# Two of four weight sums of a down projection made by copies and adding transfers in DRAM, on one core of a Trainium2 chip

## The chip, the cores and the metric

The kernel runs on one core of one Trainium2 chip. Its engines work in parallel, each through its own list of instructions in a fixed order: TensorE (PE, matrix products, with weight loads shown as PEld), VectorE (DVE), ScalarE (ACT), GpSimd (POOL) and SyncE (SP), which here does nothing but issue DMA transfers. DMA moves data between DRAM and the on-chip memory SBUF; matrix products end in PSUM, whose eight buffers are called banks. Engines wait for one another and for transfers through semaphores.

The metric is the device time of one execution in microseconds (us). Before the change it is 1109.34 us, the median of three runs (1109.31 to 1109.88).

## What is computed

One encoder block: RMSNorm, two kinds of attention (8 heads each), an output projection with residual, and a gated MLP with a small convolution, for 256 tokens and 16 meta tokens, model width 2048, MLP width 5632. All in float32. The part that the change touches is the last product, `@ w_down`:

```python
def conv_glu(x, w_gate, w_up, conv_w, conv_b, w_down):
    g = x @ w_gate
    u = x @ w_up
    ...
    gc = conv_b
    for i in range(CONV_W):
        gc = gc + conv_w[i] * gp[:, i:i + L]
    return (jax.nn.silu(gc) * u) @ w_down

def reference(x, meta_tokens, ...):
    ...
    mix = jnp.concatenate([rmsnorm(out_a, na_out_g[l]), rmsnorm(out_b, mla_out_g[l])], axis=-1)
    h = h + mix @ w_out[l]
    h = h + conv_glu(rmsnorm(h, ffn_norm_g[l]), w_gate[l], w_up[l], conv_w[l], conv_b[l], w_down[l])
    return h[:, N_META:]
```

## The kernel before

**Precision.** Each float32 operand is split into a rounded part `hi` (ACT, `split_hi`) and a rest `lo` (DVE, `split_lo`), and a product is made of three: hi·hi, hi·lo, lo·hi. So every block of weights costs one ACT and one DVE instruction before PE can use it.

**The stream of weights.** `pieces` is the list of all weight pieces in the order of use, mostly 128x1024 float32 (512 KB). `load_weights` issues their loads on SP in this order, as buffers come free: five buffers `raw` (one more, `more_raw`, in the MLP), four `whi`, four `wlo`. The pieces that belong to the scheme of seven products have their own larger buffers, two called `quarters` for the weights and two for their sums (`sums4`; these tiles carry the name quarters in the profile as well).

**The order of work.** There is no scheduler on the chip. The class `Flow` plays the whole kernel through once while it is built: each step is a generator that yields an engine and an estimated cost in ns, waits for an `Event`, or takes a buffer from `Slots`. The step that can start first is written down next. The order in which each engine's instructions are written is the order in which that engine runs them. Costs of the plan thus decide order alone; on the chip, an engine whose next instruction is not ready holds everything behind it. `load` issues a transfer and plans its end from bytes / 350 per ns, one after another, plus 2000 ns for landing.

**Stages in time.** Input and latent projections and the attention run to about 290 us, where heads of both kinds are interleaved with the projections of the next; the output projection follows (to about 400 us), then gate and up projections with their scheme of seven products (to about 870 us), then the down projection.

**POOL in the attention.** It does small things: the rest part of the meta columns of each softmax row (`meta_copies`, tile p, line 266), the split of small sums (sq8r), rotary products (kr, scr), copies of small queries (qs), and running sums of squares (sum_a, sum_b, kr). In the output projection it adds the residual (res).

**Seven products.** Half of the down projection's columns (SF = 1024) are computed by a scheme of the Strassen–Winograd kind: for each pair of 128-row blocks of the weights (`RowPair`, 22 of them) a 2x2 block product is made from seven products instead of eight. The four blocks of the weights lie in the order B11, B12, B22, B21 in `w_down_s` (512 columns each). The products 3, 2 and 1 use raw blocks; 5, 7, 6 and 4 use four sums of blocks, 512 columns each, made in `weight_sums` by DVE: the first two in one instruction of 128x1024, the other two in one of 128x512 each. `load_pair` takes a `quarters` buffer and loads the pair's 1 MB in two transfers of 512 KB, then the sums of activations (`s_down`, tile `sin`). The up projection uses the same class with a quarter of the width (q = 256 columns).

`Quarters.there` says when a piece can be split: raw pieces after `loaded`, the first two sums after `summed[0]`, the other two after `summed[1]`. A raw buffer is free again when its pieces are split and the sums made (`used("raw")`).

Of the kernel before, what the change touches and what calls it, by code (L numbers as in the profile page):

```python
# [35 lines left out]
FC = D_FF // P  # L36
# [19 lines left out]


AHEAD, BEHIND = 3, 8

# [146 lines left out]
def encoder_block(ctx: ExitStack, tc: tile.TileContext, io):  # L206
    nc = tc.nc
    ctx.enter_context(tc.manual_schedule())
    fl = Flow()
# [12 lines left out]
    def size(ap):  # L222
        n = 1
        for s in ap.shape[1:]:
            n *= s
        return n
# [13 lines left out]
    def TT(out, a, b, op):  # L240
        yield "dve", 68 + 1.04 * size(out)
        nc.vector.tensor_tensor(out, a, b, op)  # L242
# [54 lines left out]
    def one(slots):  # L297
        (t,) = yield slots, 1
        return t
# [6 lines left out]
    PW = 1024  # L306
# [89 lines left out]
    pieces = []  # L396
# [44 lines left out]
    for w, f in enumerate(QUADS):  # L441

        g, end = f // 2, (*QUADS, FC)[w + 1] // 2
# [4 lines left out]
        for i in range(KC // 2):  # L448
            r = RowPair(io["w_up_s"][w][i], i, PW // 4)
# [7 lines left out]
        for i, u in enumerate(scheme):  # L457
            a, b = (j * len(middle) // len(scheme) for j in (i, i + 1))
# [9 lines left out]
    for g in range(FC // 2):  # L468
        r = RowPair(io["w_down_s"][g], g, PW // 2)
# [13 lines left out]
    def load(out, src, ev, queue):  # L483

        nc_bytes = 4 * P * size(out)
        t = max(dma_free[0], fl.cur.t) + nc_bytes / 350.0
        dma_free[0] = t
        queue.dma_start(out, src)
        fl.set(ev, t + 2000.0 - fl.cur.t)
# [14 lines left out]
    def load_pair(r):  # L504
        if r.of == "up":
            r.raw, r.sums = yield raws, 2
        else:
            r.raw = yield from one(quarters)
        def load_S():
            if r.near:  # L510
                r.ev_S = ev_near[r.g]
                return
            r.S = yield from one(s_parts)
            src, saved = saved_sums[r.of][r.g]
            yield saved
            yield "sp", 600
            load(r.S, src, r.ev_S, nc.sync)

        if r.of == "up":
            yield from load_S()  # L520
        for a in range(0, 4 * r.q, PW):
            yield "sp", 600
            ev = r.loaded if a + PW == 4 * r.q else Event()
            load(r.raw[:, a : a + PW], r.src[:, a : a + PW], ev, nc.sync)
        if r.of == "down":
            yield from load_S()
        fl.spawn(weight_sums(r), (lambda: 0) if r.of == "up" else 2)

    def weight_sums(r):
        yield r.loaded  # L530
        if r.of == "down":
            r.sums = yield from one(sums4)
        t, raw, q = r.sums, r.raw, r.q
        yield from TT(t[:, : 2 * q], raw[:, q : 3 * q], raw[:, : 2 * q], ALU.subtract)
        fl.set(r.summed[0])
        yield from TT(t[:, 2 * q : 3 * q], raw[:, 2 * q : 3 * q], t[:, :q], ALU.subtract)
        yield from TT(t[:, 3 * q :], t[:, 2 * q : 3 * q], raw[:, 3 * q :], ALU.subtract)
        fl.set(r.summed[1])
        r.used("raw")

# [97 lines left out]
    dpool = ctx.enter_context(tc.tile_pool(name="dpool", bufs=1, space=bass.MemoryType.DRAM))  # L638
# [3 lines left out]
    }  # L642


    late = [hpool.tile([P, 2, L], F32R, tag=f"late{i}", name=f"late{i}") for i in range(8)]
    hT = [None] * KC
    s_2 = hpool.tile([P, 288], F32, name="s_2")
# [9 lines left out]
    def first_loads():  # L657
        k, first = 0, pieces[0]
        for n, weights in ((1, 1), (1, 1), (2, 2), (3, 2), (2, 1), (2, 1), (4, 2)):
            t = x_tiles[k // 8][:, k % 8 : k % 8 + n]  # L660
            yield "sp", 450
            ev = Event()
            load(t, io["xT"][:, k : k + n, :], ev, nc.sync)
            for i in range(n):
                xt[k], x_gain[k], ev_x[k] = t[:, i, :L], t[:, i, L:], ev
                k += 1
                fl.set(ev_xt[k - 1])
            if k == 1:
# [12 lines left out]
        yield "sp", 600  # L681
        load(ident, io["ident"], ev_consts, nc.sync)
        yield "sp", 600
        load(mb, io["meta_bias"], Event(), nc.sync)

    def load_residual():
        yield ev_ob[HEADS - 1]
# [291 lines left out]
    for h in range(HEADS):  # L979
        t = apool.tile([P, 2, NT], F32R, name=f"ob{h}")  # L980
        ob.append((t[:, 0, :], t[:, 1, :]))
        t = apool.tile([P, 2, NT], F32R, name=f"oa{h}") if h < 6 else hl[KC - HEADS + h]
# [817 lines left out]
    def value_sums(dst, saved, a, b, place=None):  # L1800

        (A11, A21), (A12, A22) = ((t[:, :P], t[:, P:SEQ]) for t in (a, b))

        yield from TT(A22, A21, A22, ALU.add)
        yield from TT(A21, A11, A21, ALU.subtract)
        yield from TT(A11, A22, A11, ALU.subtract)
        yield from TT(A12, A12, A11, ALU.subtract)
        parts = place
        if place is None:
            parts = yield from one(combined)  # L1810
        hl_ = parts.bitcast(F32R).rearrange("p (i t) -> p i t", i=4)
# [101 lines left out]
    sums7, sum_banks = {}, {}  # L1913
# [52 lines left out]
    def quad_out(f, P7, b):  # L1966

        out = yield from one(raws)
        U = [[out[:, (2 * i + j) * 2 * P : (2 * i + j + 1) * 2 * P] for j in range(2)] for i in range(2)]
        m = yield mts, 2  # L1970
        c, u3 = (t[:, :SEQ] for t in m)
        yield from ACT(c, P7[1], AF.Copy)
        yield from TT(U[0][0], P7[2], c, ALU.add)
        yield from TT(c, P7[6], c, ALU.add)
        yield from TT(u3, P7[7], c, ALU.add)
        fl.put(acc, b[2])
        yield from TT(U[0][1], P7[5], c, ALU.add)
        yield from TT(U[0][1], P7[3], U[0][1], ALU.add)
        fl.put(acc, b[0])
        yield from TT(U[1][1], P7[5], u3, ALU.add)  # L1980
        fl.put(acc, b[1])
        yield from TT(U[1][0], u3, P7[4], ALU.subtract)
        fl.put(acc, b[3])
        for t in m:
            fl.put(mts, t)
        for j in range(2):
            pt = yield from one(acc)
            yield from TR(
                [(pt[:, (2 * t + i) * P : (2 * t + i + 1) * P], U[i][j][:, t * P : (t + 1) * P])
                 for t in range(2) for i in range(2)]  # L1990
            )
# [15 lines left out]
    def scheme_out(sums7):  # L2007
        t = yield from one(sums4)
        c1, u2, u3 = (t[:, i * PW // 2 : (i + 1) * PW // 2] for i in range(3))
        outs = yield quarters, 2  # L2010
        C = [[o[:, j * SF // 2 : (j + 1) * SF // 2] for j in range(2)] for o in outs]

        def done(i, j):
            for k in range(2):
                o = C[i][j][:, k * 2 * P : (k + 1) * 2 * P]
                yield from ACT(o, o, AF.Copy, scale=s_2t[:, i : i + 1])
                yield from PTT(o, o, res[2 * j + k][:, i, :], ALU.add)
            yield "sp", 600
            nc.sync.dma_start(io["out"][i][:, j * SF // 2 : (j + 1) * SF // 2], C[i][j])

        yield from ACT(c1, sums7[1], AF.Copy)
        fl.put(acc, sums7[1])
        yield from TT(C[0][0], sums7[2], c1, ALU.add)
        fl.put(acc, sums7[2])
        fl.spawn(done(0, 0))
        yield from TT(u2, sums7[6], c1, ALU.add)
        fl.put(acc, sums7[6])
        yield from TT(u3, sums7[7], u2, ALU.add)
        fl.put(acc, sums7[7])
        yield from TT(C[0][1], sums7[5], u2, ALU.add)  # L2030
        yield from TT(C[0][1], sums7[3], C[0][1], ALU.add)
        fl.put(acc, sums7[3])
        fl.spawn(done(0, 1))
        yield from TT(C[1][1], sums7[5], u3, ALU.add)
        fl.put(acc, sums7[5])
        fl.spawn(done(1, 1))
        yield from TT(C[1][0], u3, sums7[4], ALU.subtract)
        fl.put(acc, sums7[4])
        fl.spawn(done(1, 0))

# [170 lines left out]
```

## Time and profile before

| | before |
|---|---|
| median of three runs | 1109.34 us |
| span of the profiled execution, first to last instruction | 1106.7 us |
| TensorE clock granted, mean | 1.000 |
| moved by DMA | 239.41 MB, 216 GB/s on average |
| ACT busy, POOL busy | 735.1 us, 140.0 us |
| 128x1024 sums of `quarters` on DVE | 22 |
| 128x512 sums of `quarters` on DVE | 44 |

The profile gives the span and not the device time of the execution it was taken from, so the difference to the median, 2.6 us, is what lies around the span.

How to read it: a group of instructions is named by source line, engine, operation and `out<-in`; `x22` is a count, then come the busy time and the mean duration of one, then the idle time of that engine just before the group and what ended it. Many operations are recorded in helpers, so that a line alone (238 for ACT, 242 for DVE, 266 for POOL, 278 for PE) says little and the tile names tell which step it is. Matmuls overlap and their ends are modelled, so PE's busy time says that work was queued, and only the spacing of the starts tells the pace. A view of waits names, for each engine, whom it waited for, with the total time, the number of times and the longest one.

### The profile page before, as it was taken

The numbers are of one execution on the slowest core, as the hardware profiler recorded it, in microseconds if no ns is written. First come the engines' busy times: TensorE is split into PE (matmuls) and PEld (weight loads), VectorE is DVE, ScalarE is ACT, GpSimd is POOL, SyncE is SP. The second block draws the span as 40 slices with busy tenths as digits, with TensorE's granted clock in tenths as the row PEclk, the third lists the DMA queues.
The fourth block names the chain that finished last, engine by engine and source line by source line (L and its number), as shares of the span: only waits on it lengthen the run. The fifth ranks groups of instructions, "written<-read, shape, count | busy, mean of one in ns | idle before, by whom it ended". The sixth has DMA issues, their size and how long they took to land.

```text
span 1106.7 us, 22544 instructions
## 1 busy us (share of the span) xinstructions
PE 1100.6 (99%) x8414; PEld 1061.8 (96%) x8414; DVE 990.8 (90%) x1837; ACT 735.1 (66%) x1470; POOL 140.0 (13%) x202
## 2 busy tenths in 40 slices
PE   9999999999999999999999999999999999999998
PEld 9999999999999999999999999999999988888888
DVE  8979888888878989999999999988988999999984
ACT  8788979798647776656666565665565565655663
POOL 3211222121433400000000000000000011100114
PEclk9999999999999999999999999999999999999999
DMA  9553434444665796657667577777688787777772
GB/s 323 199 172 124 148 127 151 139 163 134 230 188 161 207 343 229 198 181 243 224 193 230 179 248 241 238 229 244 203 275 299 260 299 250 251 258 266 281 249 77
DMA packets 72374, 239.41 MB, mean 216 GB/s; under 512 B 8136, under 2 KB 12744, under 8 KB 72264
## 3 DMA queue, kind: packets, MB, share of 16 engines
q1 hardware_dynamic: 71976, 237.69, 63.8%
q8 instruction: 66, 1.08, 0.4%
q14 instruction: 44, 0.36, 0.1%
q10 hardware_dynamic: 288, 0.27, 0.1%
HBM read 219.44 MB, written 17.83 MB: 214 GB/s over the span
## 4 chain that ended last, share of the span: by engine, by line
PE 90%; ACT 4%; DVE 3%; issue 1%; DMA 1%; POOL 0%; DVEq 0%; POOLq 0%; ACTq 0%
PE bank L278 24%; PE bank L606 18%; PE bank L607 18%; PE bank L608 18%; PE bank L1870 6%; PE bank L1871 3%; PE bank L284 2%; ACT whi L238 1%; ACT scr L238 1%; DVE wlo L242 1%; DVE scr L250 1%; DMA raw<-in_w_cq 1%; ACT qraw L238 0%; ACT bank L238 0%; DVE cols L258 0%
## 5 line engine op out<-in xcount | busy, mean ns | idle before, releaser
L238 ACT ACTIVATE whi<-raw 128x512 fp32r<-128x512 f32 (+2 forms) x479 | 358.1, 764 | 173.2 <-PE bank L607 83.5
L242 DVE TENSOR_TENSOR wlo<-raw,whi 128x512 fp32r<-128x512 f32 (+2 forms) x479 | 414.9, 885 | 43.2 <-ACT whi L238 42.1
L606 PE MATMUL bank<-hl,whi 128*128 128x258 f32 (+2 forms) x1528 | 438.5, 287 | 0.1
L607 PE MATMUL bank<-hl,whi 128*128 128x258 f32 (+2 forms) x1528 | 433.7, 284 | 0.0
L608 PE MATMUL bank<-hl,wlo 128*128 128x258 f32 (+2 forms) x1528 | 433.0, 283 | 0.2 <-DVE wlo L242 0.2
L608 PEld LDWEIGHTS bank<-hl,wlo 128*128 128x128 f32 x1528 | 290.1, 190 | 0.9 <-DVE wlo L242 0.7
L607 PEld LDWEIGHTS bank<-hl,whi 128*128 128x128 f32 x1528 | 289.6, 190 | 0.1
L606 PEld LDWEIGHTS bank<-hl,whi 128*128 128x128 f32 x1528 | 288.6, 189 | 0.5 <-ACT scr L238 0.3
L238 ACT ACTIVATE whi<-quarters 128x1024 fp32r<-128x1024 f32 x88 | 81.5, 950 | 64.8 <-PE bank L1870 46.0
L278 PE MATMUL bank<-whi,act 128*128 128x256 f32 (+1 forms) x420 | 111.5, 317 | 0.0
L1870 PE MATMUL bank<-act,whi 128*128 128x512 f32 x308 | 110.1, 397 | 0.0
L242 DVE TENSOR_TENSOR wlo<-quarters,whi 128x1024 fp32r<-128x1024 f32 x88 | 99.4, 1156 | 10.8 <-ACT whi L238 10.2
L266 POOL TENSOR_TENSOR mt<-mt,mt 128x256 f32<-128x256 f32 x7 | 6.8, 979 | 652.4 <-ACT mt L238 652.4
L1871 PE MATMUL bank<-act,wlo 128*128 128x256 f32 x308 | 86.4, 281 | 0.0
L278 PE MATMUL bank<-whi,sin 128*128 128x512 f32 (+1 forms) x272 | 83.5, 355 | 0.0
L278 PEld LDWEIGHTS bank<-whi,act 128*128 128x128 f32 x420 | 74.1, 189 | 5.7
L1870 PEld LDWEIGHTS bank<-act,whi 128*128 128x128 f32 x308 | 57.8, 188 | 13.9
L278 PE MATMUL bank<-whi,hl 128*128 128x256 f32 x288 | 66.5, 280 | 0.0
L278 PE MATMUL bank<-wlo,act 128*128 128x256 f32 (+1 forms) x210 | 66.3, 315 | 0.0
L238 ACT ACTIVATE whi<-more_raw 128x1024 fp32r<-128x1024 f32 (+2 forms) x46 | 44.1, 962 | 24.4 <-PE bank L607 9.9
L1871 PEld LDWEIGHTS bank<-act,wlo 128*128 128x128 f32 x308 | 58.1, 189 | 1.6
L278 PEld LDWEIGHTS bank<-whi,sin 128*128 128x128 f32 x272 | 49.5, 188 | 7.7
(278 smaller groups left out, 1947.9 us busy)
## 6 DMA issues: line engine op xcount, KB each, us to landing
raw<-in_w_gate SPq DMA_DIRECT2D x83, 512.0 KB, 5.0
raw<-in_w_in SPq DMA_DIRECT2D x52, 512.0 KB, 3.9
raw<-in_w_up_s SPq DMA_DIRECT2D x44, 512.0 KB, 4.9
quarters<-in_w_down_s SPq DMA_DIRECT2D x44, 512.0 KB, 6.9
raw<-in_w_up SPq DMA_DIRECT2D x34, 512.0 KB, 5.5
raw<-in_w_out SPq DMA_DIRECT2D x32, 512.0 KB, 4.0
raw<-in_w_down SPq DMA_DIRECT2D x32, 512.0 KB, 5.2
s_down<-sums SPq DMA_DIRECT2D x22, 512.0 KB, 4.1
```

The source lines that it names most:

```text
L238: nc.scalar.activation(out, in_, f, **kw)
L242: nc.vector.tensor_tensor(out, a, b, op)
L250: nc.vector.scalar_tensor_tensor(out, a, s, b, op0, op1)
L266: nc.gpsimd.tensor_tensor(out, a, b, op)
L278: nc.tensor.matmul(o, l, r, start=start, stop=stop)
L284: nc.tensor.transpose(o, i, ident[:n, :n])
L606: nc.tensor.matmul(ps, whi, xhi, start=start, stop=False)
L607: nc.tensor.matmul(ps, whi, xlo, start=False, stop=False)
L608: nc.tensor.matmul(ps, wlo, xhi, start=False, stop=stop)
L1870: nc.tensor.matmul(ps, whi, x, start=start, stop=False)
L1871: nc.tensor.matmul(ps[:, :n], wlo, x[:, 0, :], start=False, stop=stop)
```

## The change

The first two of the four weight sums of each row pair of the down projection are no longer made on DVE. During the attention, `sums_in_dram` copies the first two blocks (B11, B12) of each pair from DRAM to a DRAM tile `early` (SP's queue, 512 KB), waits for the copy, and then adds the next two (B12, B22) to it by an adding transfer issued from POOL, DRAM to DRAM (512 KB). It starts when weight piece 18 has landed and is paced by the constants 2000, 1000 and `PACE` = 5000 ns of the plan.

In the down projection, `load_pair` loads B11 (256 KB) and B22, B21 (512 KB), leaves B12 out, and `weight_sums` loads the two finished sums (512 KB) into the sums buffer through SP once that buffer is free. The other two sums are still made on DVE, from these.

An adding transfer can only add, so the signs of the scheme are turned: the sums of weights become additions, and a few operations on activations and on the results swap add and subtract. This holds for the up projection too, whose four sums stay on DVE.

```diff
+PACE = 5000.0
...
-        for a in range(0, 4 * r.q, PW):
+        q = r.q
+        for a, b in ((0, q), (2 * q, 4 * q)) if r.of == "down" else ((0, 4 * q),):
             yield "sp", 600
-            ev = r.loaded if a + PW == 4 * r.q else Event()
-            load(r.raw[:, a : a + PW], r.src[:, a : a + PW], ev, nc.sync)
+            ev = r.loaded if b == 4 * q else Event()
+            load(r.raw[:, a:b], r.src[:, a:b], ev, nc.sync)
...
         t, raw, q = r.sums, r.raw, r.q
-        yield from TT(t[:, : 2 * q], raw[:, q : 3 * q], raw[:, : 2 * q], ALU.subtract)
-        fl.set(r.summed[0])
-        yield from TT(t[:, 2 * q : 3 * q], raw[:, 2 * q : 3 * q], t[:, :q], ALU.subtract)
-        yield from TT(t[:, 3 * q :], t[:, 2 * q : 3 * q], raw[:, 3 * q :], ALU.subtract)
+        if r.of == "down":
+            yield early_sums[r.g][1]
+            yield "sp", 600
+            load(t[:, : 2 * q], early_sums[r.g][0], r.summed[0], nc.sync)
+            yield r.summed[0]
+        else:
+            yield from TT(t[:, : 2 * q], raw[:, q : 3 * q], raw[:, : 2 * q], ALU.add)
+            fl.set(r.summed[0])
+        yield from TT(t[:, 2 * q : 3 * q], raw[:, 2 * q : 3 * q], t[:, :q], ALU.add)
+        yield from TT(t[:, 3 * q :], t[:, 2 * q : 3 * q], raw[:, 3 * q :], ALU.add)
         fl.set(r.summed[1])
         r.used("raw")
...
+    early_sums = [
+        (dpool.tile([P, PW], F32, name=f"early{g}"), Event()) for g in range(FC // 2)
+    ]
+
+    def sums_in_dram():
+        for g, (t, done) in enumerate(early_sums):
+            src = io["w_down_s"][g]
+            yield "sp", 600
+            ev = Event()
+            load(t, src[:, :PW], ev, nc.sync)
+            fl.cur.t = ev.time + 2000.0
+            yield "pool", 1000
+            nc.gpsimd.dma_start(t, src[:, PW // 2 : 3 * PW // 2], accum_op=ALU.add)
+            fl.set(done, 6000.0)
+            fl.cur.t += PACE
...
         load(mb, io["meta_bias"], Event(), nc.sync)
+        yield pieces[18].loaded
+        fl.spawn(sums_in_dram())
...
-        yield from TT(A22, A21, A22, ALU.add)
+        yield from TT(A22, A21, A22, ALU.subtract)
...
-        yield from TT(A12, A12, A11, ALU.subtract)
+        yield from TT(A12, A12, A11, ALU.add)
...
-        yield from TT(U[0][1], P7[5], c, ALU.add)
+        yield from TT(U[0][1], P7[5], c, ALU.subtract)
...
-        yield from TT(U[1][1], P7[5], u3, ALU.add)
+        yield from TT(U[1][1], P7[5], u3, ALU.subtract)
...
-        yield from TT(U[1][0], u3, P7[4], ALU.subtract)
+        yield from TT(U[1][0], u3, P7[4], ALU.add)
```

The last three edits stand in the same way in the function that puts the down projection's results together.

More of the change, by code (lines that the diff above doesn't have):

```diff
@@ L2029, in scheme_out @@
         fl.put(acc, sums7[7])
-        yield from TT(C[0][1], sums7[5], u2, ALU.add)
+        yield from TT(C[0][1], sums7[5], u2, ALU.subtract)
         yield from TT(C[0][1], sums7[3], C[0][1], ALU.add)
@@ L2033, in scheme_out @@
         fl.spawn(done(0, 1))
-        yield from TT(C[1][1], sums7[5], u3, ALU.add)
+        yield from TT(C[1][1], sums7[5], u3, ALU.subtract)
         fl.put(acc, sums7[5])
         fl.spawn(done(1, 1))
-        yield from TT(C[1][0], u3, sums7[4], ALU.subtract)
+        yield from TT(C[1][0], u3, sums7[4], ALU.add)
         fl.put(acc, sums7[4])
```

## The prediction, made before the changed kernel was run

> **What bounds the kernel now.** I read the page first, then a table by stage, then who the matrix engine waits for.
>
> ```profile
> span 1106.7 us, 22544 instructions
> PE 1100.6 (99%) x8414; PEld 1061.8 (96%) x8414; DVE 990.8 (90%) x1837; ACT 735.1 (66%) x1470; POOL 140.0 (13%) x202
> PE 90%; ACT 4%; DVE 3%; issue 1%; DMA 1%; POOL 0%; DVEq 0%; POOLq 0%; ACTq 0%
> ```
>
> PE is busy for 99% of the span and makes up 90% of the chain that ended last; VectorE (DVE) is second at 90%. The sums that the change takes away are DVE work, so the question is whether PE ever waits for DVE where they stand. The table by stage (columns: window, its length, then busy time and instruction count of PE, PEld, DVE, ACT and POOL, clock, DMA share, GB/s) has the attention from 65 to 290, the output projection's first part to 345, the gated MLP to 875, the down projection to 1075 and the tail.
>
> ```profile
> 65.00:290.00 225.00, 224.14 (x1851) 221.05 (x1850) 199.70 (x537) 196.14 (x611) 47.99 (x99) 1.00 0.46 150
> 290.00:345.00 55.00, 55.00 (x458) 55.00 (x458) 41.59 (x70) 28.92 (x55) 17.82 (x20) 1.00 0.53 172
> 345.00:875.00 530.00, 530.00 (x4430) 529.54 (x4429) 491.57 (x912) 331.39 (x535) 20.90 (x14) 1.00 0.71 234
> 875.00:1075.00 200.00, 200.00 (x1000) 168.17 (x999) 189.12 (x196) 116.69 (x138) 23.43 (x18) 1.00 0.75 265
> 1075.00:1107.00 32.00, 27.80 (x194) 25.76 (x192) 15.82 (x19) 13.77 (x21) 11.18 (x11) 1.00 0.25 83
> ```
>
> In the down projection DVE is busy for 189 of 200 us, yet PE is busy for all 200. Busy PE is modelled, so the timeline (start, duration) has to confirm it:
>
> ```profile
> 1077.33 0.40 PE L1870 MATMUL bank<-act,whi 128*128 128x512 f32 x1
> ...
> 1077.56 0.28 PE L1871 MATMUL bank<-act,wlo 128*128 128x256 f32 x1
> ...
> 1077.67 0.40 PE L1870 MATMUL bank<-act,whi 128*128 128x512 f32 x1
> ```
>
> A 512-column product starts 0.23 us and a 256-column one 0.11 us before the next: 0.45 ns a column, in step. The waits of PE and of its weight loads in the whole run (total, times, longest):
>
> ```profile
> PE bank L698 <- DVE em L695: 1.1, 1, 1.1
> PE bank L278 <- POOL sq8r L266: 0.5, 2, 0.3
> PE bank L608 <- DVE wlo L242: 0.2, 1, 0.2
> ```
> ```profile
> PEld bank L278 <- POOL sq8r L266: 1.0, 3, 0.4
> PEld bank L278 <- DVE scr L250: 0.5, 2, 0.3
> ...
> PEld bank L284 <- POOL p L266: 0.3, 1, 0.3
> ```
>
> PE waited for DVE's split weights (wlo) for 0.2 us in all. What it does wait for in the attention is mostly POOL. So the removed work lies under a saturated PE, and the added work is issued from the engine that PE is closest to waiting for.
>
> **The change part by part.**
>
> *Removed:* 22 DVE sums of 128x1024, one per row pair.
>
> ```profile
> L242 DVE TENSOR_TENSOR quarters<-quarters 128x1024 f32<-128x1024 f32 x22 | 26.7, 1216 | 0.3 <-DMA quarters<-in_w_down_s 0.3
> ```
>
> 22 x 1.216 = 26.7 us of DVE, 13% of the stage, off an engine that PE does not wait for there: 0 on the path. If PE were not covering it, it would be worth at most these 26.7 us. The changed signs swap add and subtract at equal count and shape: 0. Leaving out one of four quarters takes 22 x 256 KB off the loads.
>
> *Added in the down projection:* a 512 KB load of the finished sums per pair, so net 256 KB and one SP issue more, and a wait: SP holds the load until a sums buffer is free, and the loads of raw weights queue behind it. Before, this pair's times were (first sum on DVE; first use of its result by ACT):
>
> ```profile
> 964.94 1.21 DVE L242 TENSOR_TENSOR quarters<-quarters 128x1024 f32<-128x1024 f32 x1
> ```
> ```profile
> 972.29 1.06 ACT L238 ACTIVATE whi<-quarters 128x1024 fp32r<-128x1024 f32 x1 [1.63 <-PE bank L1870]
> ```
> ```profile
> quarters<-in_w_down_s SPq DMA_DIRECT2D x40, 512.0 KB, 6.9
> ...
> sin<-s_down SPq DMA_DIRECT2D x20, 512.0 KB, 3.4
> ```
>
> Sum to use was 7.3 us, and ACT then still waited 1.6 us for PE to free a buffer. A 512 KB load lands in 3.4 us (single) to 6.9 us (in pairs); this one is single, so nearer 3.4. It fits; two DVE sums wait for it. DMA there rises from 0.75 by 0.08 (5.8 MB at the rate of the next rows). I take +0.2 us, with bounds 0 and 22 x 0.5 = 11 us if it is late in each pair.
>
> *Added in the attention:* 22 copies DRAM to DRAM on SP's queue and 22 adding transfers on POOL's, one pair about every 11.5 us by the constants of the diff (1.5 for 512 KB at the planner's 350 bytes/ns, 2 landing, 2 margin, 1 issue, 5 pace), from about 65 us for some 255 us. Two costs: the DMA engines, and POOL's time.
>
> DMA engines, 60 to 350 us, then the down projection (packets, MB, share):
>
> ```profile
> q1 hardware_dynamic: 15523, 44.36, 46.8%
> ...
> raw<-in_w_in SPq DMA_DIRECT2D x40, 512.0 KB, 3.9
> ```
> ```profile
> q1 hardware_dynamic: 16078, 54.17, 73.2%
> ```
>
> 44.36 MB took 0.468 x 290 = 136 us of all engines, 0.33 MB/us, so 1.6 us per 512 KB. A copy counts 1.6; no row shows an adding transfer, which reads two operands and writes one: bounds 1.6 (as a copy) and 4.8 (three streams). Together 22 x 3.2 to 6.4 = 70 to 141 us in some 280, a share of 0.25 to 0.50 on top of 0.46 to 0.53: 0.71 to 1.03. The MLP runs at 0.71 and the down projection at 0.73 without PE idle, and weights wait for buffers, not the reverse:
>
> ```profile
> SPq L488 <- DVE wlo L242: 158.6, 57, 5.9
> ```
>
> In that stretch SP stood 57 times, up to 5.9 us, until a raw buffer was read, so loads are issued as far ahead as buffers allow. I take two streams (3.2 us, share about 0.85): 0 us.
>
> POOL: no DMA is issued from it before. Its rows in that stretch, and one use of a POOL result:
>
> ```profile
> L266 POOL TENSOR_TENSOR p<-p 128x16 fp32r<-128x16 f32 x40 | 13.1, 330 | 52.9 <-ACT p L238 44.7 <-PE bank L607 3.5 <-PE bank L608 3.5
> L266 POOL TENSOR_TENSOR sum_b<-sum_b,scr 128x258 f32<-128x258 f32 x7 | 11.3, 1617 | 32.7 <-ACT scr L238 26.0 <-ACT p L238 5.1 <-ACT pt L238 1.5
> ```
> ```profile
> 194.26 0.22 POOL L266 TENSOR_TENSOR p<-p 128x16 fp32r<-128x16 f32 x1
> ...
> 194.54 0.49 PE L284 MATMUL bank<-ident,p 128*128 128x128 f32 x3
> ```
> ```profile
> 252.54 0.22 POOL L266 TENSOR_TENSOR p<-p 128x16 fp32r<-128x16 f32 x1
> ...
> 253.11 0.49 PE L284 MATMUL bank<-ident,p 128*128 128x128 f32 x3
> ```
>
> The softmax's last step on POOL (p) ends 0.06 and 0.35 us before PE transposes it; I use 0.2 as PE's slack. In the built order of the changed kernel the POOL instruction right behind an adding transfer is such a p 8 times, a split of small sums (sq8r) once, small queries 4 times, a rotary product once, running sums 6 times and the residual twice. Behind p or sq8r stand ACT's or PE's next step and everything on PE after it, since PE's order is fixed.
>
> How late is POOL against its plan? The plan books 1.0 us. The nearest rows for the issue are POOL's shortest and longest instructions above, 0.22 and 1.62 us; I take 1.3, nearer the long one because an issue for 128 rows is more than a 16-column subtraction: +0.3. The wait for the copy: planned 5.5 us after its issue; loads land at 3.4 to 6.9 (median rows), the copy's landing is not shown, and SP's order can delay its issue. So 0 to 1.4 us late; I take 0.7. Sum 1.0 us, bounds -0.8 (counted as no gain) and 2.0. POOL was idle 52.9/40 = 1.3 us before a p, which absorbs about half of the cases. So 9 x 0.5 x (1.0 - 0.2) = 3.6 us, and 0.4 for the five small queries and rotary steps; bounds 0 and 9 x (2.0 - 0.2) = 16.
>
> The Trainium skill (SBUF — State Buffer, "SBUF: two separate sides") says that a DMA issued from POOL gets its descriptors from POOL's cores, which cannot write them while DVE runs an instruction in a two-port mode. The row that could do it is this one:
>
> ```profile
> L246 DVE TENSOR_SCALAR p<-p,cols x40: 222/353/364, 88.1 to 281.8; 128x272 f32<-128x272 f32 x32, 4x272 f32<-4x272 f32 x4, 4x16 f32<-4x16 f32 x4
> ```
>
> One such instruction in the way of each of the nine would add 9 x 0.35 = 3.2 us, so 1116.7 by that rule; no trace of before shows it. [...]
>
> **The sum.** Against the span: 1106.7 + 3.6 + 0.4 + 0.2 = 1110.9. The median of the runs, 1109.3, is 2.6 above the span, which I keep: 1113.5.
>
> **The rivals.**
>
> All hidden. POOL issues within 1.0 us and copies land in time. For it: POOL is 13% busy, and idle 1.3 us before a p on average. Against: the slack of 0.06 us. Only reshuffling is left, 0 to +1.5: 1109.5.
>
> The DMA engines fill up. If the adding transfer costs 4.8 us, the share reaches 1.0 from 290 to 345. For it: read and write in DRAM at once, which no row shows. Against: loads far ahead. Loads would fall behind by the 0.5 x 55 = 27 us of added transfers there, less what the buffers hold: five of 512 KB, each good for 8 blocks of 3 products at 0.12 us, 14 us, less 3.9 for a landing, 10. So +17, 1126.
>
> Sums late in the down projection: each pair waits 0.5 us, 1109.3 + 11 = 1120. It decides from a landing above the 7.3 us of cover. The same load in pairs took 6.9 in the median, which speaks for it; the planner's order against it.
>
> Faster: the new POOL and SP items reshuffle the attention's fixed order. 1851 matmuls in 225 us are 121.6 ns each, against 119.6 in the MLP (530/4430), so 1851 x 2.0 = 3.7 us of looseness, if the mix is alike; closing three quarters of it gives 1106.5. It decides only where the delays above are nil. Against: visible idle is 225 - 224.14 = 0.9 us.
>
> That the change doesn't do what it says (sums still on DVE) the built order excludes: 22 fewer such instructions.
>
> **How the numbers follow.** POOL late, 1113.5 (its own range 1111.7 to 1119): 0.45. All hidden: 0.27. DMA full: 0.15. Sums late: 0.07. Faster: 0.06. What a measurement can tell from no change is about 0.2%, 2.2 us. Slower 0.45 + 0.15 + 0.07 = 0.67, same 0.27, faster 0.06. The range leaves out the faster case and the far part of DMA full: 1108 to 1128.
>
> **What would show it.** Right: 22 fewer 128x1024 sums, DVE near 162 of 200 us in the down projection with PE still at 200; PE idle in 65 to 290 up from 0.9 by some 4 us, put down to POOL p, sq8r or qs. Wrong: PE waits for ACT whi behind DMA raw in 65 to 345 (DMA full); ACT or DVE waits for DMA quarters<-early (sums late); PE idle unchanged (hidden). A copy that lands in under 5 us, or a POOL issue under 1 us, would take my forecast's ground away.

## The result, and the profile after

The changed kernel takes 1112.56 us (median of 7 runs, 1110.91 to 1113.69) against 1109.34 us for the kernel before on the same chip: a ratio of 1.0027, 95% interval 1.0017 to 1.0036. It is slower by 3.2 us; the forecast was slower by 4.2. The profiled execution took 1112.61 us, with a span of 1110.7 us, 4.0 more than before. In all seven runs of after the time lies 1.9 to 2.1 us above the span, not the 2.6 us that I took from before. By that, the profiled execution of before was some 0.6 us quicker than its median, and the spans differ by more than the medians do.

The head of the page of after:

```profile
span 1110.7 us, 22646 instructions
...
PE 1102.1 (99%) x8414; PEld 1062.1 (96%) x8414; DVE 968.0 (87%) x1815; ACT 735.1 (66%) x1470; POOL 156.5 (14%) x224
```

DVE lost 22 instructions and 22.8 us, POOL won 22 and 16.5 us, and PE has the same 8414. The table by stage of after, with the columns of the one before:

```profile
65.00:290.00 225.00, 223.02 (x1842) 219.93 (x1840) 198.84 (x535) 195.22 (x611) 62.92 (x116) 1.00 0.79 224
290.00:345.00 55.00, 55.00 (x458) 55.00 (x457) 41.55 (x72) 28.68 (x55) 20.20 (x22) 1.00 0.83 261
345.00:875.00 530.00, 530.00 (x4433) 529.70 (x4432) 491.22 (x912) 332.44 (x537) 21.04 (x14) 1.00 0.68 233
875.00:1075.00 200.00, 198.99 (x991) 166.39 (x990) 165.59 (x173) 116.38 (x138) 21.84 (x18) 1.00 0.80 290
```

PE idles 2.0 us in the attention instead of 0.9, and in the down projection, where it had no gap at all, 1.0 us. Busy PE is modelled and hides part of a stop, so the loss is better read from a landmark that both kernels have: the start of POOL's first addition of each of the six output tiles that it finishes. Three of the six, before and then after:

```profile
895.39 0.76 POOL L266 TENSOR_TENSOR mt<-mt,mt 128x256 f32<-128x256 f32 x1 [509.14 <-ACT mt L238]
...
928.58 1.24 POOL L266 TENSOR_TENSOR mt<-mt,mt 128x256 f32<-128x256 f32 x1 [29.60 <-ACT mt L238]
...
1058.50 1.24 POOL L266 TENSOR_TENSOR mt<-mt,mt 128x256 f32<-128x256 f32 x1 [29.61 <-ACT mt L238]
```
```profile
897.29 0.76 POOL L267 TENSOR_TENSOR mt<-mt,mt 128x256 f32<-128x256 f32 x1 [509.57 <-ACT mt L239]
...
931.14 1.25 POOL L267 TENSOR_TENSOR mt<-mt,mt 128x256 f32<-128x256 f32 x1 [30.79 <-ACT mt L239]
...
1062.24 1.24 POOL L267 TENSOR_TENSOR mt<-mt,mt 128x256 f32<-128x256 f32 x1 [30.77 <-ACT mt L239]
```

After is 1.90 us late by 895 us, 2.56 at the second and 3.74 at the last: 1.9 us were lost ahead of the down projection and 1.8 in it (in three steps of about 0.65); the other 0.3 of the span lies behind. Not all of the 1.9 us belongs to the change. PE runs the same products in the same order in both kernels up to 64 us, and the starts of after are already 0.8 us late at 41 us, when the first copy is issued (40.6 us); the profiles of the other runs lie between -0.4 and +0.6 us there. That leaves 1.1 us for the attention, as much as PE's idle time grew. So the loss has two places, and they have two causes.

**In the attention.** PE's waits of after, then those of its weight loads:

```profile
...
PE bank L1897 <- DVE wlo L243: 1.0, 3, 0.3
PE bank L279 <- POOL sq8r L267: 1.0, 2, 0.5
PE bank L279 <- DVE sq8r L255: 0.6, 1, 0.6
...
```
```profile
PEld bank L1897 <- DVE wlo L243: 2.3, 3, 0.8
PEld bank L279 <- POOL sq8r L267: 1.6, 4, 0.6
```

No POOL p is in either list. In the attention PE waits besides sq8r only for ACT p (0.4 us, as in the run below that has the order alone, 0.3). What stands ahead of an sq8r is seen in the timeline of after (the bracket is the idle time before the instruction and what ended it):

```profile
239.62 0.43 DVE L243 TENSOR_TENSOR scr<-scr,consts 128x258 f32<-128x258 f32 x1 [1.29 <-DMA scr<-scr]
...
239.97 0.17 DVE L255 CAST sq8r<-sq 128x8 fp32r<-128x8 f32 x1
...
240.21 0.58 POOL L267 TENSOR_TENSOR sq8r<-sq,sq8r 128x8 fp32r<-128x8 f32 x1 [1.18 <-DVE sq8r L255]
...
240.84 0.22 PE L279 MATMUL bank<-ones_r,sq8r 128*4 128x2 f32 x3 [0.49 <-POOL sq8r L267]
```

DVE stands 1.29 us at the product that reads a rotary swap (the four small SBUF-to-SBUF transfers of each rotary step, `scr<-scr`). Behind it in DVE's fixed order waits the cast that makes the high part of sq8r, behind that POOL's low part, behind that PE. The wait that the trace books on POOL begins at a DMA. The chain of waits of after has such swaps among its longest pieces (start, duration); that of before has none there:

```profile
69.72 3.93 DMA scr<-scr
115.82 4.04 DMA scr<-scr
```

Landing times from 65 to 290 us (median, last column), before and after, and DVE's waits for swaps in the whole run of before and of after:

```profile
scr<-scr SPq DMA_DIRECT2D x16, 32.2 KB, 2.3
```
```profile
scr<-scr SPq DMA_DIRECT2D x16, 32.2 KB, 5.4
```
```profile
DVE scr L242 <- DMA scr<-scr: 1.2, 1, 1.2
```
```profile
DVE scr L243 <- DMA scr<-scr: 4.3, 4, 2.2
```

**In the down projection.** The timeline of DVE and PE around the first of the three stops, in after, and DVE's rows at the same place in before:

```profile
896.23 2.37 DVE L243 TENSOR_TENSOR wlo<-quarters,whi 128x1024 fp32r<-128x1024 f32 x2
...
898.52 1.22 DVE L243 TENSOR_TENSOR quarters<-quarters,quarters 128x512 f32<-128x512 f32 x1
...
899.67 1.76 DVE L243 TENSOR_TENSOR wlo<-raw,whi 128x1024 fp32r<-128x1024 f32 x1
...
901.48 0.39 PE L1897 MATMUL bank<-act,wlo 128*128 128x256 f32 x1 [0.34 <-DVE wlo L243]
```
```profile
894.33 2.37 DVE L242 TENSOR_TENSOR wlo<-quarters,whi 128x1024 fp32r<-128x1024 f32 x2
896.68 1.70 DVE L242 TENSOR_TENSOR wlo<-raw,whi 128x1024 fp32r<-128x1024 f32 x1
```

In after a sum of the weights stands between the two low parts; in before none does. It is one of the two sums that DVE kept. It comes now because its input, the early sums, is loaded behind the raw blocks, and the planner lets it land at least 3.5 us after them (1.5 us for the bytes, 2 for landing). Here it takes 1.22 us instead of its usual 0.68, beside POOL's additions at 898.12 and 899.27 (three of the 44 such sums of after run beside a POOL addition and take 1.22 us, the other 41 at most 0.69), and the low part that PE needs next starts 1.15 us later than it could.

### The profile page after: what moved, and what is told of

Same layout as the page of the kernel before. It is cut to its first block, busy times and chain, and to the rows that moved or that the text cites. A ratio compares the mean times of both kernels' runs of the same rounds, so it can differ in the third digit from the quotient of the medians.

```text
span 1110.7 us, 22646 instructions
## 1 busy us (share of the span) xinstructions
PE 1102.1 (99%) x8414; PEld 1062.1 (96%) x8414; DVE 968.0 (87%) x1815; ACT 735.1 (66%) x1470; POOL 156.5 (14%) x224
## 4 chain that ended last, share of the span: by engine, by line
PE 90%; ACT 4%; DVE 3%; DMA 2%; issue 1%; POOL 0%; SPq 0%; DVEq 0%; ACTq 0%; POOLq 0%
PE bank L279 23%; PE bank L614 19%; PE bank L615 19%; PE bank L616 19%; PE bank L1896 6%; PE bank L1897 3%; PE bank L285 2%; DVE wlo L243 2%; ACT whi L239 1%; ACT scr L239 1%; DMA scr<-scr 1%; DMA raw<-in_w_cq 1%; DVE quarters L243 0%; ACT bank L239 0%; SPq L489 0%
```

## The experiments

Eight of the kernels (those with "attention" below) keep the down projection of before, by this edit of the changed kernel, so that only the attention differs; nothing reads the DRAM buffers in them. The orders of PE, DVE and ACT are the same in the first seven.

```diff
-for a, b in ((0, q), (2 * q, 4 * q)) if r.of == "down" else ((0, 4 * q),):
+for a, b in ((0, 2 * q), (2 * q, 4 * q)) if r.of == "down" else ((0, 4 * q),):
...
-        if r.of == "down":
...
-            load(t[:, : 2 * q], early_sums[r.g][0], r.summed[0], nc.sync)
-            yield r.summed[0]
-        else:
...
+        yield from TT(t[:, : 2 * q], raw[:, q : 3 * q], raw[:, : 2 * q], ALU.add)
...
```

The kernels were run in four groups, each with the kernel before beside it on the same chip. Its median was 1108.70 to 1108.88 us there, against 1109.34 beside after, so medians of two groups are not compared as they stand. The ratios are taken over all runs of a group and not from the medians. The last column is for the whole execution; it and the landing times are of one profile each.

| run | median us | ratio to before, 95% interval | swaps land (median us, 65 to 290) | DVE waits for swaps, us |
|---|---|---|---|---|
| attention: order only | 1108.21 | 0.9995 [0.9986, 1.0004] | 2.4 | 0.8 |
| attention: copies only | 1108.59 | 0.9998 [0.9989, 1.0007] | 4.2 | 2.1 |
| attention: copies and adding transfers | 1109.95 | 1.0010 [1.0001, 1.0018] | 5.5 | 3.9 |
| attention: adding transfers only | 1110.17 | 1.0023 [1.0013, 1.0034] | 4.5 | 5.4 |
| attention: tiny adding transfers | 1108.33 | 0.9995 [0.9986, 1.0004] | 2.3 | 0.5 |
| attention: two copies for each adding transfer | 1108.86 | 1.0002 [0.9993, 1.0011] | 3.5 | 1.9 |
| attention: adding transfers, swaps unread | 1108.00 | 0.9993 [0.9984, 1.0002] | 5.1 | none |
| down projection only | 1110.67 | 1.0016 [1.0007, 1.0025] | 2.5 | 1.3 |
| changed kernel, early load first | 1110.77 | 1.0018 [1.0009, 1.0027] | 5.6 | 4.9 |
| same, transfers during the MLP | 1124.62 | 1.0145 [1.0131, 1.0159] | 2.3 | 1.5 |
| early load first, swaps planned later | 1116.67 | 1.0071 [1.0057, 1.0084] | 4.2 | none |
| attention: swaps planned later, no transfers | 1114.65 | 1.0053 [1.0040, 1.0066] | 2.6 | none |

**Attention or down projection?** First the attention with all its transfers (the edit above and no other), then the down projection alone:

> Copies and adding transfers run in the attention as in the changed kernel, but the down projection loads all four blocks again and makes all four sums on DVE (the sums in DRAM are made and not read). PE's and ACT's orders are those of the changed kernel. If the loss of 3.2 us comes half from the attention and half from the down projection, as the gaps between PE's starts say (about 1.9 and 1.8 us more than before): 1111.0, PE idle in 65 to 290 about 2.0 us as after, the three stops near 900, 966 and 1032 gone. If it comes from the attention alone: 1112.5. If from the down projection alone: 1109.3.

```diff
-        yield pieces[18].loaded
-        fl.spawn(sums_in_dram())
...
-            yield early_sums[r.g][1]
...
-            load(t[:, : 2 * q], early_sums[r.g][0], r.summed[0], nc.sync)
+            load(t[:, : 2 * q], r.src[:, :PW], r.summed[0], nc.sync)
```

> No transfers in the attention and its order as before; the down projection as in the changed kernel (22 sums fewer, block 1 not loaded, turned signs), with the early sums' buffer filled from the first half of the weights themselves, so the same bytes land but the sums are not those of the reference. TensorE's order is that of before. Theory A (the down projection costs what the profile of after shows there): about 1.8 us over before, 1110.5 us, with three stops of TensorE of about 0.6 us each, behind a VectorE low part that stands behind a sum of the weights; TensorE busy 199.0 of 200 us in 875 to 1075. Rival (my forecast: 0.2 us there, and the three stops in after came from the attention's shift): within 0.5 us of before, TensorE busy 199.8 or more.

Their excesses of 0.10% and 0.16% add up to 0.26%, against the change's 0.27%; each is known to about 0.09%, so that they agree so closely is partly luck. The row of the down projection in the run of it alone, and PE's waits:

```profile
875.00:1075.00 200.00, 198.99 (x990) 166.40 (x990) 164.89 (x171) 116.44 (x137) 21.82 (x18) 1.00 0.82 291
```
```profile
PE bank L1894 <- DVE wlo L243: 1.0, 3, 0.3
```

The same three waits as in after, with PE's order that of before: the cost is the down projection's own, and not a shift handed on by the attention.

**Order, copies, adding transfers.** Three runs leave out one or both of the transfers, and keep their places in the plan:

```diff
-            load(t, src[:, :PW], ev, nc.sync)
+            dma_free[0] = max(dma_free[0], fl.cur.t) + 4 * P * PW / 350.0
+            fl.set(ev, dma_free[0] + 2000.0 - fl.cur.t)
...
-            nc.gpsimd.dma_start(t, src[:, PW // 2 : 3 * PW // 2], accum_op=ALU.add)
```

(both for the order only; the second alone for the copies only; the first alone for the adding transfers only)

> As e1_transfers_only, but neither a copy nor an adding transfer is issued; the plan books them, so PE, DVE and ACT keep the same order. If only the order that the plan writes costs time: as e1_transfers_only, about 1111.0. If the transfers themselves cost it, by POOL or by traffic: 1109.3 +- 0.5, swaps landing 2.7 us again.

> As e1_transfers_only, with the 22 adding transfers left out (the sums in DRAM are not finished, and not read) and the orders of PE, DVE, ACT and SP unchanged. If POOL, held behind the copies, makes the attention's loss (the forecast): as e4_order_only, within 0.4 us of it. If the copies' traffic makes it, by making the small swaps of the rotary step late (landing 2.7 before, 5.6 after): as e1_transfers_only within 0.4, swaps landing above 4 us and DVE still waiting for them.

> As e1_transfers_only, with the 22 copies left out: the adding transfers go onto what lies in DRAM (not read), and POOL has no copy to wait for; same orders. If POOL's hold behind the copies (33 us in 12 waits) makes the loss: as e4_order_only, 1109.3. If traffic of either kind makes it: between e4_order_only and e1_transfers_only, with swaps landing between 2.7 and 5.6 us; POOL's issue 0.83 us each in any case.

The order costs nothing that can be measured, the copies neither. The adding transfers alone cost at least as much as the pair (the intervals overlap), though POOL then waits for no copy: it waited 36 us in after and not at all here. Its rows in after (the waits; then the issue, with min/median/max in ns):

```profile
POOL early L665 <- DMA early<-in_w_down_s: 35.9, 13, 6.4
```
```profile
L665 POOL DMA_DIRECT2D early<-in_w_down_s x20: 809/830/862, 73.2 to 325.3; - x20
```

So POOL's hold behind the copies, which my forecast rested on, is not needed for the loss. The 11 runs with the adding transfers alone spread from 1109.27 to 1114.66 us, the order only from 1107.29 to 1108.72: what the transfers cost changes from run to run. The profile is of a run of 1110.17 us; none shows the slowest.

PE's order is the same in after and in the run with the order only, so the same product can be followed from one to the other. Around the largest step, order only and then after:

```profile
120.96 0.28 PE L610 MATMUL bank<-hl,wlo 128*128 128x258 f32 x1
121.26 0.17 PE L279 MATMUL bank<-ones_r,sq8r 128*4 128x2 f32 x1
```
```profile
122.21 0.28 PE L616 MATMUL bank<-hl,wlo 128*128 128x258 f32 x1
123.07 0.17 PE L279 MATMUL bank<-ones_r,sq8r 128*4 128x2 f32 x1 [0.57 <-DVE sq8r L255]
```

After goes from 1.25 to 1.81 us behind at this product, which reads an sq8r, and from 1.92 to 2.52 at the one of 240.84 us shown above. Between 66 and 846 us it falls back by 1.8 us in all; against before it shows as 1.1, since the new order by itself is some 0.7 us quicker there in its profile. In the same stretch the run with both transfers falls back by 1.1 us, with adding transfers only by 2.7, with copies only by 0.4.

**Issue or traffic?** The tiny run moves 16 of the 1024 columns and issues as much; the other leaves POOL out and moves the bytes in two plain copies. Neither has the copies of the change.

```diff
-            load(t, src[:, :PW], ev, nc.sync)
+            dma_free[0] = max(dma_free[0], fl.cur.t) + 4 * P * PW / 350.0
+            fl.set(ev, dma_free[0] + 2000.0 - fl.cur.t)
...
-            nc.gpsimd.dma_start(t, src[:, PW // 2 : 3 * PW // 2], accum_op=ALU.add)
+            nc.gpsimd.dma_start(t[:, :16], src[:, PW // 2 : PW // 2 + 16], accum_op=ALU.add)
```

> Attention as in the run with adding transfers alone, every instruction in the same place on every engine, but each adding transfer moves 16 of its 1024 columns; the down projection is that of before. GpSimd still issues 22 adding transfers, the traffic is 1/64. Theory A (the adding transfers cost by their traffic: the rotary swaps land late, VectorE waits for them, the small queries' parts come late): the time falls to that of the order alone, 1108.2 to 1108.6 us; swaps land in 2.5 us in the median again. Rival (the 0.83 us that GpSimd spends on each issue makes its p and sq8r late): the time stays at 1110 us, with TensorE's idle time put down to GpSimd.

```diff
...
-            nc.gpsimd.dma_start(t, src[:, PW // 2 : 3 * PW // 2], accum_op=ALU.add)
+            for u in extra[g]:
+                nc.sync.dma_start(u, src[:, PW // 2 : 3 * PW // 2])
```

> Attention as in the run with adding transfers alone, but in the place of each adding transfer SyncE issues two plain copies of the same bytes into DRAM; GpSimd issues nothing. The down projection is that of before. Two copies took the 16 engines about as long as one adding transfer. Theory A (traffic, whoever issues it): as slow as the adding transfers alone, 1109.7 to 1110.3 us, rotary swaps landing at 4.5 us or more in the median. Rival (GpSimd's issue time): 1108.2 to 1108.6 us although the DMA engines are as busy.

The issues remain in the tiny run (0.82 us in the median of 20, against 0.83), and the time is that of the order: it is the traffic. The two copies fell between the theories: the engines were about as busy (share 0.71 from 65 to 290 us, against 0.68 with adding transfers), the swaps landed in 3.5 us instead of 4.5, and the time is within 0.1% of before. So a share of busy engines doesn't tell the cost. Neither does the landing of the swaps in the median: 5.5 us with both transfers goes with 1.0010, 4.5 with adding transfers only with 1.0023, 4.2 with copies only with 0.9998. What goes with the cost in the first seven rows is the last column, how long DVE stood at swaps: up to 2.1 us no loss can be told, at 3.9 and 5.4 us there is one. Why an adding transfer delays swaps more than two copies, these runs leave open.

**Are the swaps the link?** The same run with adding transfers, but the swaps go where nothing reads them:

```diff
+        junk = dpool.tile([P, L], F32, name=f"junk{n_junk[0]}")
...
-            load(tmp[i * half : (i + 1) * half, :n], t[j * half : (j + 1) * half], swapped, nc.sync)
+            load(junk[i * half : (i + 1) * half, :n], t[j * half : (j + 1) * half], swapped, nc.sync)
...
-        yield from TT(tmp[:, :n], tmp[:, :n], const("sin", n), ALU.mult)
+        yield from TT(tmp[:, :n], t, const("sin", n), ALU.mult)
```

> As the run with adding transfers alone (1110.17 us), every instruction in the same place on every engine, but the rotary swaps land in DRAM, where nothing reads them, and VectorE multiplies the tile that was to be swapped: the swaps are still issued, the adding transfers still run, and nothing waits for a swap (the rotated halves are not those of the reference). Theory A (swaps that land late hold VectorE, which makes the small queries' parts late for TensorE): the time falls to 1108.2 to 1108.7 us although the DMA engines are as busy; TensorE's waits for VectorE's and GpSimd's sq8r shrink to a few tenths. Rival (the adding transfers delay something else, such as the weights' loads or GpSimd): 1109.5 us or more.

The swaps land no earlier than with the swaps read (5.1 us against 4.5), and the loss is gone, from 1.0023 to 0.9993. PE's waits for sq8r with the adding transfers alone, and with the swaps unread:

```profile
PE bank L279 <- DVE sq8r L255: 1.6, 3, 0.7
PE bank L279 <- POOL sq8r L267: 1.2, 3, 0.5
```
```profile
PE bank L279 <- POOL sq8r L267: 0.5, 1, 0.5
```

All that was changed is where the swaps land and that DVE doesn't wait for them; every engine's order is the same. For the adding transfers alone this shows the chain: swap late, DVE held, sq8r late, PE idle. For the pair of after the same chain is read from its trace. Unread swaps without any transfers were not run as a control; the order only, whose DVE stands 0.8 us at swaps, leaves little for them to gain.

**The place of the early load.** One edit of the changed kernel:

```diff
+        if r.of == "down":
+            fl.spawn(load_early(r))
         for a, b in ((0, q), (2 * q, 4 * q)) if r.of == "down" else ((0, 4 * q),):
...
+    def load_early(r):
+        r.sums = yield from one(sums4)
+        yield early_sums[r.g][1]
+        yield "sp", 600
+        load(r.sums[:, : 2 * r.q], early_sums[r.g][0], r.summed[0], nc.sync)
...
-            r.sums = yield from one(sums4)
+            yield r.summed[0]
...
-            load(t[:, : 2 * q], early_sums[r.g][0], r.summed[0], nc.sync)
...
```

> The changed kernel with one edit: the early sums of a weight group are loaded ahead of its raw blocks and not behind them, so that the two sums left to VectorE can come as early as in the kernel before. TensorE's order is that of the changed kernel. Theory A (the down projection's three stops come from sums that stand later in VectorE's order because their load is planned behind the raw blocks): 1.2 to 1.8 us faster than the changed kernel, 1110.8 to 1111.3 us, and no stop of TensorE over 0.3 us between 875 and 1075. Rival (the stops come from the split work itself, whatever the load's place): 1112.0 to 1112.8 us with stops of 0.6 us.

The stage and DVE at the place of the stop:

```profile
875.00:1075.00 200.00, 199.87 (x995) 167.22 (x994) 167.09 (x176) 116.42 (x138) 21.84 (x18) 1.00 0.84 295
```
```profile
894.29 3.50 DVE L243 TENSOR_TENSOR wlo<-quarters,whi 128x1024 fp32r<-128x1024 f32 x3
897.76 1.71 DVE L243 TENSOR_TENSOR wlo<-raw,whi 128x1024 fp32r<-128x1024 f32 x1
```

No sum stands between the low parts any more, and PE is short of 0.13 us instead of 1.01. The median lies 1.8 us below that of after, but in another group: over its own before it is 2.0 us, where after is 3.2, and the ratio falls by 0.09%, 1.0 us, less than was expected. The two intervals overlap, so the stage's row carries this verdict. By PE's starts, against the run "attention: copies and adding transfers", which has the same PE order, the down projection loses 0.75 us instead of 1.7: the place of the load explains some 1.0 us of it, and three smaller steps behind a wlo remain (at 933, 998 and 1064 us), which no run takes away.

**Two repairs that failed.** Both start from the kernel with the early load first. The first moves the transfers into the MLP, where there are no swaps:

```diff
-PACE = 5000.0
+PACE = 14000.0
...
-        yield pieces[18].loaded
+        yield ev_mlp
         fl.spawn(sums_in_dram())
```

> The changed kernel with the early sums loaded ahead of the raw blocks, and with the copies and adding transfers made after the attention (from about 345 us, 14 us of pace in the place of 5), where no swap waits. TensorE's order is that of the kernel before; VectorE still has 22 sums fewer. Theory A (the loss lies in the swaps of the attention and in the place of the sums' load): 1108.2 to 1109.0 us, the time of before within 0.1%, with TensorE busy 530 of 530 in 345 to 875 and 199.8 of 200 in 875 to 1075; no gain, since TensorE had nothing to win there. Rival (the transfers delay the weights' loads of the MLP, DMA share 0.66 to 0.70 there without them): 1110 us or more, TensorE's idle time between 345 and 875 above 0.5 us, behind ACT or VectorE that wait for raw.

The second plans the swaps to land 3 us later; its control has the down projection of before and no transfers:

```diff
-    def load(out, src, ev, queue):
+    def load(out, src, ev, queue, more=0.0):
...
-        fl.set(ev, t + 2000.0 - fl.cur.t)
+        fl.set(ev, t + 2000.0 + more - fl.cur.t)
...
-            load(tmp[i * half : (i + 1) * half, :n], t[j * half : (j + 1) * half], swapped, nc.sync)
+            load(tmp[i * half : (i + 1) * half, :n], t[j * half : (j + 1) * half], swapped, nc.sync, 3000.0)
```

> The changed kernel with the early sums loaded ahead of the raw blocks (1110.77 us) and one more edit: the planner takes a rotary swap to land 3 us later than it did, so that VectorE's reader of the swap is ordered behind the sq8r casts and not ahead of them. All transfers of the change stay in the attention. Theory A (the loss in the attention is VectorE standing at the swap): 1108.5 to 1109.6 us, within 0.1% of before, with VectorE's waits for swaps under 1.5 us in all. Rival (the new order loses elsewhere, for it moves hundreds of instructions): 1110 us or more, with the idle time of TensorE in 65 to 290 us put down to other operands than sq8r.

> The control of the run with swaps planned later: the same planning of the attention, with neither copies nor adding transfers issued, and the down projection of before. Theory A: the order alone is worth 1107.8 to 1108.7 us, as the order alone was before (1108.2), and the run with the transfers lies within 0.7 us of it. Rival (the order planned with later swaps is itself worse): 1109.5 us or more.

In the MLP the rival won, and by far: 15.7 us slower than before. The stage, and ACT's waits for the gated MLP's weights:

```profile
345.00:875.00 530.00, 521.45 (x4323) 517.50 (x4322) 477.37 (x880) 320.15 (x520) 38.39 (x35) 1.00 0.83 266
```
```profile
ACT whi L239 <- DMA raw<-in_w_up: 19.0, 8, 4.3
ACT whi L239 <- DMA raw<-in_w_gate: 13.0, 6, 4.6
```

In after these two were 3.2 and 4.4 us and PE had no gap. At a share of 0.83 the MLP's loads come late, while the stretch from 290 to 345 us carries the same 0.83 in after with PE at 55.00 of 55.00: that lasts 55 us, this 530. What the new places of the transfers in the plan cost without traffic was not run.

With the swaps planned later, DVE waits for none, but the time is 8.0 us above before, and the control without transfers is 5.9 us above it already: its attention has PE at 219.76 of 225 us.

```profile
65.00:290.00 225.00, 219.76 (x1804) 215.36 (x1803) 195.79 (x525) 190.94 (x594) 49.74 (x95) 1.00 0.43 140
```

PE stands there for other operands (ACT p 1.4 us, DVE pt 1.3, ACT scr 1.2), so the rival holds: the attention has no 3 us to give. The two runs were expected within 0.7 us of each other and lie 2.0 apart. PE's order is the same in both, and by its starts the two profiles part by 1.1 us in the attention, without any wait of DVE for a swap (and by 0.4 in the MLP and 0.9 in the down projection). So in that order the transfers reach PE by another way as well. The largest step is a product that waits for ACT (PE's waits for ACT qraw are 1.1 us instead of 0.5); the trace leads from there to a rotary product on POOL that took 2.24 us instead of 1.81, but no run tests it. No version found is measurably faster than the kernel before.

## Why the prediction was right, and where it was not

The sign and the size came out: 1112.56 us against 1113.5, and the span of 1110.7 us against a sum of 1110.9. The sum's terms did not: 4.0 us for POOL that no run shows stand against 1.1 us at the swaps and 1.6 more than I took in the down projection. That they nearly cancel is luck, and so is the close agreement of the span, of which 0.8 us was lost ahead of the first copy.

- *What bounds it, and the removed sums at 0:* right (the lines that I showed for PE's pace, at 1077 us, come after the stage, but at 1030 us the starts are as close, 0.24 and 0.11 us). DVE lost 22.8 us and nothing became faster. Where DVE has 34 us to spare in the down projection (165.59 of 200), PE can still wait for it, for what counts is where an instruction stands in DVE's order and not how full the engine is.
- *Changed signs at 0:* right as part of the order only (0.9995).
- *POOL late, 3.6 + 0.4 us:* this step failed, and what the runs showed in its place is the wait for the swaps. The planned 1.0 us for the issue was above the 0.83 that it takes, so the +0.3 was none. The wait for the copy was there (36 us, longest 6.4), since copies land in 6.4 us; but in this order it cost nothing that a run shows: without the hold the loss stayed, and with the swaps unread it went while POOL issued as before. No POOL p became a wait of PE. POOL still waited for p's input 54.5 us, 32 times in after, so there was more cover than the half that I took.
- *DMA engines at 0:* the price of the transfers was right, the conclusion only for the weights. I took 3.2 us an adding transfer; the adding queue's share with adding transfers alone was 24.4% of 225 us for 17 transfers, 3.2 us each. A copy, from the share of the plain queue with and without (56.8 less 45.7%, 18 copies), took 1.4 against my 1.6, and 1.6 in the run with two copies (70.3 less 45.7%, 34 copies). The share came to 0.79 and 0.83 against 0.85, and no weight was late. But I asked only who waits for weights. The swaps landed in 5.4 us instead of 2.3, and a swap that an engine reads straight ahead of PE's input has no buffers loaded far ahead. That is where the attention's loss went: 1.8 us of this profile against the order alone, 1.1 against before.
- *Down projection, 0.2 us:* mis-sized, 1.8 measured. I asked whether the load would land in time, and it did (DVE waited 2.1 us for it in all, in small pieces). The place of the sums that follow it in DVE's order, moved by the load's planned time, is what cost some 1.0 us of it; the rest is open.
- *The rivals:* "all hidden" is out by the interval (1.0017 and above). "Engines fill up" did not happen in the attention, and did when the transfers were put into the MLP. "Sums late" had the right stage with another mechanism and 1.8 us, not 11. The order alone was 0.5 us quicker in the median, which can't be told from none.
- *What would show it:* half held. The 22 sums were gone and DVE stood at 166 of 200 us in the down projection, but PE was at 199.0 there and not at 200. The idle time of PE in 65 to 290 us grew by 1.1 us, not 4, and it was put down to sq8r as I wrote, from POOL among others; but its start was a swap. The rule "an issue under 1 us would take my ground away" applied, and I had the right time with the ground gone.

## What to carry to other kernels

Before moving work to idle DMA engines, list the small transfers on which an engine stands in order, and not only the big loads: big loads have buffers ahead of them, a swap has nothing. A wait that the trace books on one engine (here POOL sq8r) is followed back until an instruction waited for something outside its own chain; here that took two more steps, to a DMA. And when a planner sets the order, moving an input's planned time moves the instructions behind it, so ask what then stands ahead of the tightest operand. Where two runs have the same order on PE, the starts of the same products show where time is lost, and how much of a difference was there before the change could act (here 0.8 us).

## What was not expected of the hardware

- An adding transfer of 512 KB in DRAM used 3.2 us of the 16 engines, a copy 1.4 to 1.6; they landed in 7.6 and 6.4 us in the median of after, and the adding transfer held up swaps more than two copies of its bytes did (4.5 against 3.5 us).
- The issue of an adding transfer on POOL took 809 to 862 ns in 20 cases, with DVE busy for 88% of the stage. The Trainium skill (SBUF — State Buffer, "SBUF: two separate sides") has descriptors wait while DVE is in a two-port mode. The trace hardly tries this: one issue alone overlapped an instruction of the row that the prediction named (at 281.85 us), and its 862 ns are the longest of the 20, 32 above the median. Moving 8 KB in the place of 512 left the issue at 0.82 us.
- A 128x512 sum on DVE took 1.22 us instead of 0.68, and a 128x1024 low part 1.76 instead of 1.22, beside POOL's additions. The second is there in before as well (1.70 at 896.68 us), harmless as long as nothing else stands ahead of it.
